# An encoder trunk on one core: the SSD mixer on a normalised residual, a scan in eight lagging steps, and aligned pools

## The chip, the cores and the metric

The kernel runs on one core of a Trainium2 chip. The metric is the device time of one execution in microseconds (us). Five engines work side by side, each through its own instructions in order: PE (TensorE, matmuls; its weight loads are listed as PEld), DVE (VectorE), ACT (ScalarE), POOL (GpSimd) and SP, which issues the transfers. An instruction waits by semaphores for what other engines make.

## The reference

Two layers on a residual `h` of 512 tokens by 1024 numbers, all in float32:

```
for i in range(2):
    h = h + 0.5 * swiglu(rmsnorm(h, g1), w_gu1, w_down1)          # FFN1, inner width 2816
    hn = rmsnorm(h, g_mix)
    h = h + (ssd_mixer(hn) if i == 0 else neighbourhood_attention(hn))
    h = h + 0.5 * swiglu(rmsnorm(h, g2), w_gu2, w_down2)          # FFN2
    h = h + sigmoid(rmsnorm(h, gp) @ w_gate) * rmsnorm(p[i] @ w_proj, gq)   # gated embedding

ssd_mixer(hn):
    z, xbc, dt = split(hn @ w_in)                  # 8256 columns
    xbc = silu(conv5(xbc) + conv_b)                # a centred convolution of 5 taps, each channel by itself
    xs, b_f, c_f, b_b, c_b = split(xbc)            # 32 heads of 64, 8 groups of 128 for B and C
    y = scan(xs, dt_f, b_f, c_f) + scan backwards(xs, dt_b, b_b, c_b) + d * xs
    return rmsnorm(y * silu(z), g) @ w_out

scan, in chunks of 128 tokens:
    y = (C B^T * exp(cum_q - cum_k), masked) @ (x dt)             # within a chunk
    states of a chunk = B^T @ (x dt * exp(cum_end - cum))
    carried = carried * exp(cum_end) + states                     # from chunk to chunk
    y += (C @ carried) * exp(cum)                                 # across chunks
```

## The kernel before

The residual lies as eight tiles `hs` of 128 channels by 512 tokens. Each product with a weight is cut into units: a unit is a piece of 128 by up to 1024 of the weight that makes 128 outputs for all tokens. `load_unit` fetches it (tile `wr`), `split_unit` splits it into a high part (`wh`, a cast on ACT, L157) and a low part (`wl`, DVE, L159), three units ahead. The operand is split in the same way by `split`: a high part on ACT (L181, L178) and a low part on DVE (L182, L179), side by side in one tile of two rows of 2048 bytes, `xa` or `md`. `gemm` adds three matmuls of 512 columns for each 128 inputs: L172 high by high, L173 high by low, L174 low by high. A unit with 8 inputs has 24 matmuls.

`Norm` feeds `h * gain` to the products, and the row factor R = 1/sqrt(mean of squares) multiplies what comes out. Squares are made on ACT (L201) and added up on POOL (L205). `SumSq.rsqrt` sums over the partitions with one matmul of ones (L209, 512 columns in plain float32), and three Newton steps on DVE work on 128 by 512 numbers (L187 to L193, L211).

In the SSD, `conv` takes the bank that a unit left in PSUM times R into SBUF (L413), multiplies the middle tap on ACT (L416), adds the four others on DVE (L420), then tanh on ACT (L423) and a product on DVE (L424). Units 6 and 7 of a group make the gate z in the same manner (L437 to L440). There are eight groups of heads, eight units to each. `scan(gi)` works on one group, and yields between its steps; the loop at the end of `ssd` runs the units of the next group (`project(gi + 1)`, with the last group the first half of the output product, `out_half`) and takes one step after each unit. Its products on PE are: C B^T (L459), transposes of xs and B (L470), the chunks' states (L518), the products within chunks (L539) and those with the carried states (L556). POOL makes x dt (L478), that with its decay (`xds`, L486), the masked products (L501) and sums (L560); DVE carries the states on (L525, L526). The Tile framework orders every engine's instructions at build time, by priority and by what it takes to be ready.

The SSD's exit adds the second half of the output product (L608 DVE, L609 POOL, L613 DVE into a new `hs` tile), and each tile goes at once into the next norm (L181, L182, L201, L205). The gated embedding is `ple` (L326 to L330). The output leaves by L835.

The tiles come from pools that lie one behind the other in each partition of SBUF: 16384 bytes for transfers' descriptors, the constants `cp` (8608 bytes), the weights `wp`, the data `bp`. All weight and data tiles of a row or more are multiples of 2048 bytes, apart from `sm` at 32 bytes.

## Time and profile before

| | |
|---|---|
| Three executions | 2464.87, 2467.52, 2467.38 us; median 2467.38 |
| Span of the profiled execution | 2462.0 us from its first to its last instruction |
| Around the span | the profiled execution has no time of its own beside its span; the median of the three lies 5.4 us above it |
| Granted TensorE clock | 0.992 on the mean |

How to read it: times in the profile are microseconds from the start of the span unless marked ns. In the list of groups, a row names line, engine, operation, the tiles written and read, the shape, the count, then busy time in us, the mean in ns, and the idle time of the engine just before with what ended it. The list of waits names who waited for whom: us in total, times, the longest. A window's row has its length, then busy time with the number of instructions (x) for PE, PEld, DVE, ACT and POOL, then the granted clock of PE, the share of the transfers' engines and GB/s. A row of the timeline has the start, the length, engine and line, and in brackets the idle time before and what ended it.

The stages by time: FFN1 to 375 us, the SSD to 987, FFN2 and the gated embedding to 1415, FFN1 of the second layer to 1785, attention to 2049, then FFN2 and the embedding.

### The profile page before, as it was taken

The numbers are of one execution on the slowest core, as the hardware profiler recorded it, in microseconds if no ns is written. First come the engines' busy times: TensorE is split into PE (matmuls) and PEld (weight loads), VectorE is DVE, ScalarE is ACT, GpSimd is POOL, SyncE is SP. The second block draws the span as 40 slices with busy tenths as digits, with TensorE's granted clock in tenths as the row PEclk, the third lists the DMA queues.
The fourth block names the chain that finished last, engine by engine and source line by source line (L and its number), as shares of the span: only waits on it lengthen the run. The fifth ranks groups of instructions, "written<-read, shape, count | busy, mean of one in ns | idle before, by whom it ended". The sixth has DMA issues, their size and how long they took to land. (4 is left out here: it accounts for less than half of the span.)

```text
span 2462.0 us, 29096 instructions
## 1 busy us (share of the span) xinstructions
PE 2395.0 (97%) x11278; PEld 1953.4 (79%) x11278; DVE 1548.6 (63%) x1983; ACT 964.0 (39%) x1545; POOL 489.4 (20%) x387
## 2 busy tenths in 40 slices
PE   8999999999999999899999999999999999999998
PEld 6888888777777778788888778888877878888887
DVE  6553448888888866645344964444478965553457
ACT  4322234555555563332234432222336753322242
POOL 2110110545555543211012111101100011110120
PEclk9999999999999999999999999999999999999999
DMA  4333342533443354233333333333434323333332
GB/s 165 96 96 100 90 126 89 167 119 122 125 123 120 122 174 129 87 101 94 96 102 95 95 93 99 99 94 92 139 120 125 112 67 99 96 94 99 99 94 77
DMA packets 89562, 266.60 MB, mean 108 GB/s; under 512 B 10944, under 2 KB 11584, under 8 KB 89424
## 3 DMA queue, kind: packets, MB, share of 16 engines
q1 hardware_dynamic: 89424, 264.75, 35.5%
q8 instruction: 88, 1.44, 0.2%
q14 instruction: 50, 0.41, 0.1%
HBM read 253.93 MB, written 10.78 MB: 108 GB/s over the span
## 5 line engine op out<-in xcount | busy, mean ns | idle before, releaser
L172 PE MATMUL ps<-xa,wh 128*128 128x512 f32 x2216 | 877.9, 396 | 17.9 <-ACT xa L181 9.2
L173 PE MATMUL ps<-xa,wh 128*128 128x512 f32 x2216 | 870.7, 393 | 3.3 <-DVE xa L182 3.3
L174 PE MATMUL ps<-xa,wl 128*128 128x512 f32 x2216 | 869.1, 392 | 0.0
L157 ACT CAST wh<-wr 128x1024 fp32r<-128x1024 f32 (+1 forms) x405 | 418.4, 1033 | 1027.2 <-PE ps L173 638.8
L159 DVE TENSOR_TENSOR wl<-wr,wh 128x1024 fp32r<-128x1024 f32 (+1 forms) x405 | 588.8, 1454 | 126.4 <-ACT wh L157 121.0
L172 PEld LDWEIGHTS ps<-xa,wh 128*128 128x128 f32 x2216 | 419.7, 189 | 108.0 <-ACT xa L181 10.6
L173 PEld LDWEIGHTS ps<-xa,wh 128*128 128x128 f32 x2216 | 419.7, 189 | 97.2 <-issue 7.1
L174 PEld LDWEIGHTS ps<-xa,wl 128*128 128x128 f32 x2216 | 418.9, 189 | 88.5 <-DVE wl L159 1.2
L172 PE MATMUL ps<-md,wh 128*128 128x512 f32 x960 | 376.6, 392 | 1.2 <-ACT md L181 1.2
L173 PE MATMUL ps<-md,wh 128*128 128x512 f32 x960 | 374.0, 390 | 1.1 <-DVE md L182 1.1
L174 PE MATMUL ps<-md,wl 128*128 128x512 f32 x960 | 373.5, 389 | 0.0
L257 POOL TENSOR_TENSOR t<-t,sc 128x512 f32<-128x512 f32 x88 | 121.2, 1379 | 1025.4 <-ACT wh L157 735.0
L205 POOL TENSOR_TENSOR sq<-sq,sq 128x512 f32<-128x512 f32 x77 | 112.0, 1454 | 595.8 <-ACT sq L201 594.6
L256 DVE TENSOR_TENSOR t<-ps,rt 128x512 f32<-128x512 f32 x88 | 60.8, 690 | 255.5 <-PE ps L174 255.5
L172 PEld LDWEIGHTS ps<-md,wh 128*128 128x128 f32 x960 | 180.2, 188 | 41.2 <-ACT md L181 2.4
L173 PEld LDWEIGHTS ps<-md,wh 128*128 128x128 f32 x960 | 180.2, 188 | 40.4 <-DVE md L182 2.3
L267 DVE SCALAR_TENSOR_TENSOR hs<-ps,hs 128x512 f32<-128x512 f32 x96 | 66.2, 690 | 229.7 <-PE ps L174 229.7
L174 PEld LDWEIGHTS ps<-md,wl 128*128 128x128 f32 x960 | 180.2, 188 | 37.6
L420 DVE SCALAR_TENSOR_TENSOR t<-t,ccw,t 128x510 f32<-128x510 f32 (+1 forms) x192 | 178.8, 934 | 5.3 <-ACT t L416 2.8
L252 DVE TENSOR_TENSOR t<-ps,rt 128x512 f32<-128x512 f32 x88 | 60.8, 691 | 127.4 <-PE ps L174 127.2
L501 POOL TENSOR_TENSOR sc<-sc,sc 128x512 f32<-128x512 f32 x64 | 106.7, 1688 | 29.8 <-ACT sc L500 29.8
L178 ACT CAST md<-t 128x512 fp32r<-128x512 f32 x88 | 54.9, 624 | 120.5 <-POOL t L257 120.5
(154 smaller groups left out, 1771.3 us busy)
## 6 DMA issues: line engine op xcount, KB each, us to landing
wr<-in_w_gu_dram SPq DMA_DIRECT2D x176, 512.0 KB, 3.6
wr<-in_w_in_dram SPq DMA_DIRECT2D x65, 512.0 KB, 3.6
wr<-in_w_dn_dram SPq DMA_DIRECT2D x64, 448.0 KB, 3.3
wr<-in_w_dn_dram SPq DMA_DIRECT2D x32, 512.0 KB, 3.5
hs<-crow SPq DMA_DIRECT2D x64, 256.0 KB, 3.6
wr<-in_w_qkv_dram SPq DMA_DIRECT2D x24, 512.0 KB, 3.6
hs<-vrow SPq DMA_DIRECT2D x64, 128.0 KB, 3.0
wr<-in_w_out_dram SPq DMA_DIRECT2D x16, 512.0 KB, 4.0
```

What stands on the lines that cost most here:

```text
L157: s.copy(out=hi[:, :n], in_=raw[:, :n])
L159: v.tensor_sub(out=lo[:, :n], in0=raw[:, :n], in1=hi[:, :n])
L172: te.matmul(out=pt, lhsT=hi[:, sl], rhs=xp[:, 0, :], start=first and k == 0, stop=False)
L173: te.matmul(out=pt, lhsT=hi[:, sl], rhs=xp[:, 1, :], start=False, stop=False)
L174: te.matmul(out=pt, lhsT=lo[:, sl], rhs=xp[:, 0, :], start=False, stop=last and k == n - 1)
L205: (v if fast else g).tensor_add(out=self.acc, in0=self.acc, in1=q)
L252: v.tensor_mul(out=gm, in0=pg, in1=R[0])
L256: v.tensor_mul(out=um, in0=pu, in1=R[0])
L257: g.tensor_mul(out=um, in0=um, in1=sg)
L267: v.scalar_tensor_tensor(out=h[d], in0=pt, scalar=0.5, in1=h[d], op0=ALU.mult, op1=ALU.add)
L420: v.scalar_tensor_tensor(out=a[:, lo:hi], in0=xb[:, lo + o:hi + o], scalar=w(j), in1=a[:, lo:hi], op0=ALU.mult, op1=ALU.add)
L501: g.tensor_mul(out=e, in0=e, in1=cbm[dr])
```

## The change

- **Pools.** The descriptors get 1024 bytes. `sm` has a pool of its own ahead of the weights (12 tiles of 32 bytes), and 2272 bytes are filled in, so that `wp` begins at byte 12288 = 6 × 2048. In before it begins at 16384 + 8608 = 24992, which is 416 beyond 12 × 2048, and every tile of weights and operands lies 416 beyond a multiple of 2048. `xa` takes its tiles from `md` (24 together, as many as before), and `sc` has 15 tiles instead of 9.
- **Row factor.** `begin` and `end` make R with the tokens on the partitions: four matmuls of one column, Newton steps on 128 by 4 numbers, and four matmuls of 128 columns that spread it out again, copied by ACT. The SSD's entry and exit and both gated embeddings use it.
- **SSD on the normalised residual.** Eight new pairs `xn` hold h · gain · R. The step-size unit and the first three units of group 0 still use the old pairs; all others use `xn`, and their `conv` and gate read the PSUM bank itself.
- **Scan.** The steps stand in a new order, one after each unit: transposes and C B^T; xds; nothing on PE; states; within chunks for heads 0 and 1; across for these; across for heads 2 and 3; within for these. The exponentials (`expo`, ACT) and masks (`masked`, POOL) are spread over the steps. The last group's y stays on the chip (`late`).
- **Exit** with three gemms ahead of the first output; **gated embedding** with its first gate after the second unit, the very last unit in two halves of the columns; **start** with half weight tiles of two units and their gemms taken in turns, the squares queued behind the last cast.

```diff
+SCRATCH = 1024
+FILL = 12288 - 10016
...
+    sp = ctx.enter_context(tc.tile_pool(name="sp", bufs=12))
+    fp = ctx.enter_context(tc.tile_pool(name="fp", bufs=1))
+    v.memset(fp.tile([P, FILL // 4], F32, name="fill")[:, :1], 0.0)
...
-    hs, t2, sc, sq = slot("hs", 8), slot("t2", 7), slot("sc", 9), slot("sq", 4)
+    hs, t2, sc, sq = slot("hs", 8), slot("t2", 7), slot("sc", 15), slot("sq", 4)
     def md(dt=F32):
-        return bp.tile([P, 2, T], dt, name=nm("md"), tag="md", bufs=16)
+        return bp.tile([P, 2, T], dt, name=nm("md"), tag="md", bufs=24)
     def xa(dt=F32R):
-        return bp.tile([P, 2, T], dt, name=nm("xa"), tag="xa", bufs=8)
+        return md(dt)
...
+        def begin(self, scale=1.0, eps=EPS):
+            pt = px_bank()
+            for c in range(NC):
+                te.matmul(out=pt[:, c:c + 1], lhsT=self.acc[:, c * P:(c + 1) * P], rhs=ones_d[:, :1],
+                          start=True, stop=True)
+            m, a, self.y = sm([NC]), sm([NC]), sm([NC])
+            v.tensor_scalar(out=m, in0=pt[:, :NC], scalar1=scale, scalar2=eps, op0=ALU.mult, op1=ALU.add)
+            newton_rsqrt(m, self.y, a)
+        def end(self):
+            pt = px_bank()
+            for c in range(NC):
+                te.matmul(out=pt[:, c * P:(c + 1) * P], lhsT=self.y[:, c:c + 1].to_broadcast([P, P]), rhs=ident,
+                          start=True, stop=True)
+            r = rt()
+            s.copy(out=r, in_=pt)
+            return r
...
     def ple(l, norm, pp, nxt):
+        halves = (slice(0, T // 2), slice(T // 2, T))
+        def gate(n, pt, R, cs):
+            u = t2()[:, cs]
+            v.tensor_mul(out=u, in0=pt, in1=R[:, cs])
+            s.activation(out=u, in_=u, func=AF.Tanh)
+            v.scalar_tensor_tensor(out=u, in0=u, scalar=1.0, in1=pp[n][:, cs], op0=ALU.add, op1=ALU.mult)
+            v.tensor_add(out=h[n][:, cs], in0=h[n][:, cs], in1=u)
         R = None
         for n in range(KD):
+            if n == KD - 1 and nxt is done:
+                w = unit()
+                for x, cs in enumerate(halves):
+                    pt = mm_bank()
+                    gemm(pt[:, cs], w, norm.pairs, cols=cs)
+                    gate(n, pt[:, cs], R, cs)
+                    (sy, s)[x].dma_start(out=out[:, n, cs], in_=h[n][:, cs])
...
-                R = norm.factor(half=True)
...
+            if n == 0:
+                norm.begin(half=True)
+                held = pt
+                continue
+            if n == 1:
+                R = norm.end()
+                gate(0, held, R, slice(0, T))
+                nxt(0)
...
-        R = norm.factor()
-        Rh = rt()
-        v.tensor_scalar(out=Rh, in0=R, scalar1=0.5, scalar2=None, op0=ALU.mult)
+        norm.begin()
+        pt0, w0 = mm_bank(), unit()
+        gemm(pt0, w0, norm.pairs[:5], last=False)
+        R = norm.end()
+        gemm(pt0, w0, norm.pairs[5:], first=False, off=5)
...
+        xn = []
+        for k in range(KD):
+            t = t2()
+            v.scalar_tensor_tensor(out=t, in0=hk[k], scalar=col(norm.gain + k), in1=R, op0=ALU.mult, op1=ALU.mult)
+            xn.append(md(F32R))
+            split(xn[k], t, None)
...
-        def conv(pt, ct, dst):
-            xb = t2()
-            v.tensor_mul(out=xb, in0=pt, in1=R)
+        def conv(src, ct, dst, raw):
+            if raw:
+                xb = t2()
+                v.tensor_mul(out=xb, in0=src, in1=R)
+                src = xb
...
-                v.scalar_tensor_tensor(out=a[:, lo:hi], in0=xb[:, lo + o:hi + o], scalar=w(j), in1=a[:, lo:hi],
+                v.scalar_tensor_tensor(out=a[:, lo:hi], in0=src[:, lo + o:hi + o], scalar=w(j), in1=a[:, lo:hi],
                                        op0=ALU.mult, op1=ALU.add)
-            th = xb
+            th = t2()
...
+                raw = gi == 0 and i < 3
+                if gi == 0 and i == 0:
+                    pt = pt0
+                else:
+                    pt = mm_bank()
+                    gemm(pt, unit(), norm.pairs if raw else xn)
                 if i < 6:
-                    conv(pt, cts[i], dsts[i])
+                    conv(pt, cts[i], dsts[i], raw)
...
+                    s.activation(out=th, in_=pt, func=AF.Tanh, scale=0.5)
+                    v.scalar_tensor_tensor(out=zt[:, i - 6, :], in0=th, scalar=1.0, in1=pt, op0=ALU.add, op1=ALU.mult)
...
+        def expo(gi, j):
+            hd, dr = 4 * gi + j // 2, j % 2
+            cb = hs()
+            sy.dma_start(out=cb, in_=crow[dr, hd:hd + 1, :].to_broadcast([P, T]))
+            e = sc()
+            for c in range(NC):
+                s.activation(out=e[:, cs(c)], in_=cb[:, cs(c)], func=AF.Relu, scale=-1.0,
+                             bias=cum[:, dr, c, hd:hd + 1])
+            s.activation(out=e, in_=e, func=AF.Exp, scale=-1.0)
+            return e
+        def scan(gi, bt, ct_, xt, zt, e0):
             h0 = 4 * gi
...
+            es = [e0]
+            def masked(j):
+                g.tensor_mul(out=es[j], in0=es[j], in1=cbm[j % 2])
...
+            es.append(expo(gi, 1))
+            yield
             xds = []
...
+            masked(0)
+            masked(1)
+            es.append(expo(gi, 2))
+            masked(2)
             yield
-            es = decay(h0)
+            es.append(expo(gi, 3))
+            masked(3)
...
+            es.append(expo(gi, 4))
+            masked(4)
+            yield
+            def within(j):
...
+            def across(j):
...
+            def gated(j, y, parts):
+                for rg, vb in parts:
                     g.tensor_add(out=y[:, rg], in0=y[:, rg], in1=vb[:, rg])
                 v.tensor_mul(out=y, in0=y, in1=zt[:, j, :])
-                sy.dma_start(out=ydram[2 * gi + j], in_=y)
                 ss.add(y)
-                yield
+                if gi == NG - 1:
+                    late.append(y)
+                else:
+                    sy.dma_start(out=ydram[2 * gi + j], in_=y)
+            y = within(0)
+            es.append(expo(gi, 5))
+            masked(5)
+            yield
+            gated(0, y, across(0))
+            es.append(expo(gi, 6))
+            masked(6)
+            yield
+            es.append(expo(gi, 7))
+            masked(7)
+            parts = across(1)
+            yield
+            gated(1, within(1), parts)
+            yield
+        late = []
...
+        e0 = expo(0, 0)
         for gi in range(NG):
             beside = project(gi + 1) if gi + 1 < NG else out_half()
-            sn = scan(gi, *cur)
-            for r in beside:
+            sn = scan(gi, *cur, e0)
+            for i, r in enumerate(beside):
                 cur = r
-                next(sn, None)
-            list(sn)
         prs = pairs_of(range(8, 16), lambda: md(F32R))
+        pts = []
+        r2 = None
         for d in range(KD):
-            pt = mm_bank()
-            gemm(pt, unit(), prs)
+            while len(pts) < 3 and d + len(pts) < KD:
+                pts.append(mm_bank())
+                gemm(pts[-1], unit(), prs)
+                if r2 is None and len(pts) == 2:
+                    ss.begin(0.5, 4.0 * EPS)
+            if r2 is None:
+                r2 = ss.end()
+            pt = pts.pop(0)
...
+    begun = [(next(todo),) + tuple(wp.tile([P, 1024], dt, name=nm(t), tag=t, bufs=b)
+                                   for t, dt, b in (("wr", F32, 4), ("wh", F32R, 3), ("wl", F32R, 3)))
+             for _ in range(2)]
...
-        if k in (1, 3):
-            load_unit()
+        if k in (0, 3):
+            for src, raw, hi, lo in begun:
+                sy.dma_start(out=raw[:, wcols[k // 3]], in_=src[:, wcols[k // 3]])
...
+    def first(pg, pu, pairs):
+        for k in range(KD):
+            for pt, (src, raw, hi, lo) in zip((pg, pu), begun):
+                gemm(pt, (hi, lo), pairs[k:k + 1], first=k == 0, last=k == KD - 1, off=k)
+        with tc.issue_after(n.last_cast.ins):
+            for k in range(KD):
+                n.count(k)
```

Three places show the order. PE in group 0 of the scan, where the products with the carried states stand (md_2609 is C, md_3198 and md_3209 the carried states, L539 the products within chunks, L172 to L174 the next unit's gemm). Before:

```order
L539 MATMUL ps_3293<-sc_3150,md_3077 64x128
L539 MATMUL ps_3293<-sc_3227,md_3077 64x128
L556 MATMUL ps_3312<-md_2609,md_3198 128x128 x2
L556 MATMUL ps_3312<-md_2609,md_3209 128x128
L556 MATMUL ps_3321<-md_2609,md_3209 128x128
L556 MATMUL ps_3321<-md_2609,md_3198 128x128 x2
L172 MATMUL ps_3334<-xa_2277,wh_3160 128x512
L173 MATMUL ps_3334<-xa_2277,wh_3160 128x512
```

After, where L650 is the product with the carried states, L629 (not in these rows) that within chunks, and L177 to L179 are the gemm:

```order
L178 MATMUL ps_3404<-md_2695,wh_3272 128x512
L179 MATMUL ps_3404<-md_2695,wl_3274 128x512
L650 MATMUL ps_3444<-md_2700,md_3309 128x128 x2
L650 MATMUL ps_3444<-md_2700,md_3320 128x128
L650 MATMUL ps_3452<-md_2700,md_3320 128x128
L650 MATMUL ps_3452<-md_2700,md_3309 128x128 x2
L177 MATMUL ps_3475<-md_2660,wh_3339 128x512
L178 MATMUL ps_3475<-md_2660,wh_3339 128x512
```

L650 no longer stands directly behind the products within chunks but behind a whole unit. In the same listing the first product of the states (L608, before L518) of groups 1 to 7 stands 49 gemm matmuls behind the last transposes, in group 0 it stands 24 behind them; before it stood 29 behind them in every group.

POOL in group 1. Before, L478 makes x dt, L486 the xds, L501 the masked products:

```order
L478 TENSOR_TENSOR md_3613<-md_3612,md_2600 128x256 x2
L486 TENSOR_TENSOR sc_3643<-md_3613,md_2600 128x256
L478 TENSOR_TENSOR md_3613<-md_3612,md_2600 128x256 x2
L478 TENSOR_TENSOR md_3631<-md_3630,md_2600 128x256 x4
L486 TENSOR_TENSOR sc_3646<-md_3613,md_2600 128x256
L486 TENSOR_TENSOR sc_3643<-md_3631,md_2600 128x256
L486 TENSOR_TENSOR sc_3646<-md_3631,md_2600 128x256
L486 TENSOR_TENSOR sc_3649<-md_3631,md_2600 128x256
L486 TENSOR_TENSOR sc_3649<-md_3613,md_2600 128x256
L501 TENSOR_TENSOR sc_3695<-sc_3695,sc_3598 128x512
L501 TENSOR_TENSOR sc_3704<-sc_3704,sc_3605 128x512
```

After, L562, L584 and L547 are the same in this order; L659 and L211 are sums of the group before:

```order
L659 TENSOR_TENSOR sc_3593<-sc_3593,hs_3527 128x384
L211 TENSOR_TENSOR sq_3463<-sq_3463,sq_3598 128x512
L562 TENSOR_TENSOR md_3652<-md_3651,md_2651 128x256 x4
L562 TENSOR_TENSOR md_3670<-md_3669,md_2651 128x256 x4
L547 TENSOR_TENSOR sc_3536<-sc_3536,sc_3687 128x512
L584 TENSOR_TENSOR sc_3744<-md_3652,md_2651 128x256
L584 TENSOR_TENSOR sc_3744<-md_3670,md_2651 128x256
L584 TENSOR_TENSOR sc_3747<-md_3652,md_2651 128x256
L584 TENSOR_TENSOR sc_3747<-md_3670,md_2651 128x256
L584 TENSOR_TENSOR sc_3750<-md_3670,md_2651 128x256
L584 TENSOR_TENSOR sc_3750<-md_3652,md_2651 128x256
L547 TENSOR_TENSOR sc_3698<-sc_3698,sc_3694 128x512
```

One masked product, which needs C B^T from DVE, now stands ahead of the xds, and all of x dt ahead of both.

DVE at the SSD's entry. Before, the Newton steps of R and then the first convolution:

```order
L159 TENSOR_TENSOR wl_2658<-wr_2493,wh_2656 128x1024
L191 TENSOR_TENSOR sc_2584<-rt_2585 128x512
L192 SCALAR_TENSOR_TENSOR sc_2584<-sc_2584,sc_2583 128x512
L193 SCALAR_TENSOR_TENSOR rt_2585<-sc_2584,rt_2585 128x512
L348 TENSOR_SCALAR rt_2598<-rt_2585 128x512
L358 TENSOR_TENSOR t_2604<-ps_2550,rt_2585 64x512
L413 TENSOR_TENSOR t_2643<-ps_2612,rt_2585 128x512
L159 TENSOR_TENSOR wl_2699<-wr_2551,wh_2697 128x1024
L413 TENSOR_TENSOR t_2684<-ps_2653,rt_2585 128x512
L420 SCALAR_TENSOR_TENSOR t_2645<-t_2643,ccw,t_2645 128x510
```

After, the end of the small Newton steps, then the new pairs (L429 the product, L184 the low part), then the first product with R of a raw unit (L486):

```order
L199 SCALAR_TENSOR_TENSOR sm_2600<-sm_2599,sm_2600 128x4
L423 TENSOR_TENSOR t_2655<-ps_2562,rt_2640 64x512
L429 SCALAR_TENSOR_TENSOR t_2658<-hs_78,cst,rt_2640 128x512
L429 SCALAR_TENSOR_TENSOR t_2663<-hs_79,cst,rt_2640 128x512
L184 TENSOR_TENSOR md_2660<-t_2658,md_2660 128x512
L184 TENSOR_TENSOR md_2665<-t_2663,md_2665 128x512
L184 TENSOR_TENSOR md_2695<-t_2693,md_2695 128x512
L486 TENSOR_TENSOR t_2703<-ps_2613,rt_2640 128x512
L164 TENSOR_TENSOR wl_2719<-wr_2563,wh_2717 128x1024
L494 SCALAR_TENSOR_TENSOR t_2705<-t_2703,ccw,t_2705 128x510
```

Sixteen instructions stand between R and the first convolution where none stood; eleven of them are not shown here.

More of the change, by code (lines that the diff above doesn't have):

```diff
@@ L91, in trunk @@
     warm = cp.tile([P, 1], F32, name="warm")
-    s.activation(out=warm, in_=ones_d[:, 0:1], func=AF.Silu)
     ident = msk[:, M_ID:M_ID + P]
@@ L165, in unit, with gemm @@
         return ready.pop(0)
-    def gemm(pt, w, pairs, first=True, last=True, off=0):
+    def gemm(pt, w, pairs, first=True, last=True, off=0, cols=slice(0, T)):
         hi, lo = w
@@ L171, in gemm @@
             sl = slice((off + k) * P, (off + k + 1) * P)
[L172 to L174 removed]
+            te.matmul(out=pt, lhsT=hi[:, sl], rhs=xp[:, 0, cols], start=first and k == 0, stop=False)
+            te.matmul(out=pt, lhsT=hi[:, sl], rhs=xp[:, 1, cols], start=False, stop=False)
+            te.matmul(out=pt, lhsT=lo[:, sl], rhs=xp[:, 0, cols], start=False, stop=last and k == n - 1)
     def split(dst, src, gain):
         if gain is None:
[L178 removed]
+            cast = s.copy(out=dst[:, 0, :], in_=src)
             v.tensor_sub(out=dst[:, 1, :], in0=src, in1=dst[:, 0, :])
         else:
[L181 removed]
+            cast = s.activation(out=dst[:, 0, :], in_=src, func=AF.Copy, scale=gain)
             v.scalar_tensor_tensor(out=dst[:, 1, :], in0=src, scalar=gain, in1=dst[:, 0, :],
                                    op0=ALU.mult, op1=ALU.subtract)
+        return cast
     def newton_rsqrt(m, y, a):
@@ L225, in prep @@
             pr = self.alloc()
-            split(pr, h[k], col(self.gain + k))
+            self.last_cast = split(pr, h[k], col(self.gain + k))
             self.pairs.append(pr)
@@ L232, in count, with factor, begin, end @@
             self.ss.add(h[k], fast=k == KD - 1)
-        def factor(self, half=False):
+        def factor(self):
+            return self.ss.rsqrt()
+        def begin(self, half=False):
             if half:
-                return self.ss.rsqrt(4.0, 4.0 * EPS)
-            return self.ss.rsqrt()
-    def ffn(norm, nxt, between=lambda: None):
+                self.ss.begin(4.0, 4.0 * EPS)
+            else:
+                self.ss.begin()
+        def end(self):
+            return self.ss.end()
+    def ffn(norm, nxt, between=lambda: None, first=None):
         R = [None]
         mids = {}
+        held = []
         def gate_up(f):
-            pg = mm_bank()
+            pg, pu = mm_bank(), mm_bank()
+            if first and f == 0:
+                first(pg, pu, norm.pairs)
+                held.append((f, pg, pu))
+                return
             gemm(pg, unit(), norm.pairs)
-            pu = mm_bank()
             gemm(pu, unit(), norm.pairs)
@@ L479, in scan @@
                                  in1=bc4(dtk[:, c, dr * 32 + h0:dr * 32 + h0 + 4]))
+            cbm = []
+            for dr in range(2):
+                pt = px_bank()
+                for c in range(NC):
+                    te.matmul(out=pt[:, cs(c)], lhsT=bt[:, dr, cs(c)], rhs=ct_[:, dr, cs(c)], start=True, stop=True)
+                m = sc()
+                mk = (M_LE, M_GE)[dr]
+                v.tensor_mul(out=m.rearrange("p (c q) -> p c q", c=NC), in0=pt.rearrange("p (c q) -> p c q", c=NC),
+                             in1=msk[:, mk:mk + P].unsqueeze(1).to_broadcast([P, NC, P]))
+                cbm.append(m)
+            es.append(expo(gi, 1))
+            yield
             xds = []
@@ L539, in scan @@
                             te.matmul(out=pd[hh * 64:(hh + 1) * 64, cs(c)], lhsT=xdt[c][:, o:o + 64],
-                                      rhs=both[hh][dr][:, cs(c)], start=dr == 0 and c == 0,
+                                      rhs=es[4 * j + 2 * hh + dr][:, cs(c)], start=dr == 0 and c == 0,
                                       stop=dr == 1 and c == NC - 1)
@@ L568, in pairs_of @@
             for k in ks:
-                yt = t2()
-                sy.dma_start(out=yt, in_=ydram[k])
+                if k < 14:
+                    yt = t2()
+                    sy.dma_start(out=yt, in_=ydram[k])
+                else:
+                    yt = late[k - 14]
                 pr = alloc()
@@ L847, in trunk @@
         n.prep(k, False)
-        if k in (1, 3):
-            split_unit()
-    for k in range(KD):
-        n.count(k)
+        if k in (0, 3):
+            for src, raw, hi, lo in begun:
+                sl = wcols[k // 3]
+                s.copy(out=hi[:, sl], in_=raw[:, sl])
+                last_lo = v.tensor_sub(out=lo[:, sl], in0=raw[:, sl], in1=hi[:, sl])
+    def first(pg, pu, pairs):
[5 more added lines that the diff above has]
+                n.count(k)
     for i in range(stop):
@@ L857, in trunk @@
         if w == 0:
-            ffn(n, nxt)
+            ffn(n, nxt, first=first if i == 0 else None)
         elif w == 1:
```

78 lines of the change are left out of this document (24 added, 54 removed).

## The prediction

> **What bounds the kernel now.** I read the head of the page first, then the waits of PE, then windows and the timeline at the places they name.
>
> ```profile
> span 2462.0 us, 29096 instructions
> PE 2395.0 (97%) x11278; PEld 1953.4 (79%) x11278; DVE 1548.6 (63%) x1983; ACT 964.0 (39%) x1545; POOL 489.4 (20%) x387
> ...
> L172 PE MATMUL ps<-xa,wh 128*128 128x512 f32 x2216 | 877.9, 396 | 17.9 <-ACT xa L181 9.2
> L172 PE MATMUL ps<-md,wh 128*128 128x512 f32 x960 | 376.6, 392 | 1.2 <-ACT md L181 1.2
> ...
> PE ps L556 <- DVE md L526: 23.0, 14, 2.0
> PE ps L518 <- POOL sc L486: 12.2, 14, 1.4
> PE ps L172 <- ACT xa L181: 9.2, 4, 4.5
> ```
>
> PE is the bound. L172 runs 2216 + 960 = 3176 times, L173 and L174 as often: 9528 matmuls of 512 columns. The rest can only come from three places: how long one matmul takes, the waits, and the clock. Windows (PE first, then PEld, DVE, ACT, POOL, the clock) price one matmul and one group of the SSD scan:
>
> ```profile
> 2060.00:2400.00 340.00, 340.00 (x1500) 281.17 (x1499) 167.74 (x170) 108.76 (x137) 44.62 (x33) 1.00 0.33 97
> 448.23:514.39 66.16, 61.14 (x325) 49.68 (x324) 55.08 (x65) 34.48 (x69) 31.62 (x28) 0.95 0.40 122
> 514.39:577.80 63.41, 58.39 (x325) 47.46 (x324) 55.14 (x65) 34.48 (x69) 32.91 (x29) 1.00 0.41 125
> 464.27:471.10 6.83, 5.84 (x18) 4.97 (x19) 6.83 (x10) 4.83 (x12) 2.63 (x2) 0.50 0.40 118
> ```
>
> In a stretch of gemms alone PE takes 340/1500 = 226.67 ns each, so 9528 × 0.22667 = 2160 us of the span. A group of the scan takes 63.4 us, or 66.2 where 6.83 us of it run at clock 0.50.
>
> **The waits in the scan.** One group:
>
> ```profile
> 450.25 2.29 PE L518 MATMUL ps<-sc,md 128*128 128x256 f32 x8 [1.42 <-POOL sc L486]
> 452.85 0.70 PE L518 MATMUL ps<-sc,md 128*128 128x256 f32 x2 [0.32 <-POOL sc L486]
> 463.27 0.71 PE L556 MATMUL ps<-md,md 128*128 128x128 f32 x4 [2.00 <-DVE md L526]
> ```
>
> L518 and L556 wait 23.0 + 12.2 = 35.2 us, 5.03 in each of seven groups. After the change the states' products stand two units behind their transposes from the second group on. POOL's work in between:
>
> ```profile
> L501 POOL TENSOR_TENSOR sc<-sc,sc 128x512 f32<-128x512 f32 x56 | 94.4, 1706 | 29.8 <-ACT sc L500 29.8
> L478 POOL TENSOR_TENSOR md<-md,md 128x256 f32<-128x256 f32 x55 | 48.5, 908 | 77.2 <-ACT md L474 77.2
> L486 POOL TENSOR_TENSOR sc<-md,md 128x256 f32<-128x256 f32 x42 | 33.9, 831 | 0.0
> L474 ACT COPY md<-ps 128x512 f32<-128x512 f32 x25 | 12.8, 592 | 0.0
> ```
>
> The last transposes are followed by a copy (0.6), two xdt products (1.8), one mask (1.7, itself waiting for DVE's masked product) and six xds (5.0): 9.1 us, against 48 gemm matmuls, 10.9 us: no wait, with 1.8 us to spare. In the first group only one unit (5.4 us) lies between; the first pair of xds is ready by then, the next two come 1.7 us apart for products of 0.4, so 2.5 us stay. The carried-state products (L556, L650 after) now stand a whole unit behind the within-chunk products and wait for nothing. Waits: −35.2 + 2.5 = −32.7; between −35.2 and, if POOL's lag stays everywhere, −23.0. PE's number of changes between scan products and gemm stays (about seven a group), +0.5.
>
> **The clock.** The stretch at 0.50 follows the group's 2.00 + 1.28 us of waiting and costs 66.16 − 63.41 = 2.75 us; it comes in every second group, four times. Without the waits three go and the first group's may stay: −8.2, between −11 and 0. The Trainium skill ("TensorE: Matmul & The Clock Gate", Part 1) gives a free-running window of 3413 ns, after an idle one of which the clock halves; the 6.83 us seen is two of these, and the trace agrees.
>
> **Alignment.** All tiles of the weight and data pools start, in before, 416 bytes beyond a multiple of 2048, that is 32 beyond one of 128; after it, on a multiple of 2048 (the sizes ahead of them, from the code). No row shows an aligned moving operand. What rows show is when a matmul costs more than its columns:
>
> ```profile
> 467.56 0.63 PE L173 MATMUL ps<-xa,wh 128*128 128x512 f32 x1
> 469.27 0.63 PE L174 MATMUL ps<-xa,wl 128*128 128x512 f32 x1
> ...
> 380.44 1.02 PE L209 MATMUL ps<-sq,ones_d 128*128 128x512 f32 x2
> ...
> L209 PE MATMUL ps<-sq,ones_d x2: 591/592/592, 380.4 to 380.9; 128*128 128x512 f32 x2
> ```
>
> The first two rows are the first and the last of five matmuls in a row in the stretch at clock 0.50: 1.71/4 = 0.427 us from one to the next, so 213.5 ns at full clock if columns were all. The fast matmul has 13 ns on top of that, and 226.67 is 17/16 of 213.33 (the 512 columns at 2.4 a ns that 0.427 us at half clock come to) to the hundredth. The plain float32 L209 pair, 1.02 − 0.59 = 0.43 us from one to the next, twice 213.5 and no more, also has nothing on top. Both take in 512 columns at half the pace. So the extra sixteenth appears only where the operand is read at the full pace: a limit of its supply, not of the array. A row of 2048 bytes that starts 32 beyond a multiple of 128 touches 17 pieces of 128 bytes, an aligned one 16. That fits without a free number; a fixed start-up of the read of just a sixteenth fits too, and would stay. Bounds: 0 and −13.3 ns for each of 9528, 0 to −127 us. I take the near end of the half-pace rows, with their 1.7 to 2 ns on top of 2 × 213.3 for an instruction: 215.3, so −11.3 × 9528 = −108. About 3.5 us of that are lost where PE waits for others (the SSD's exit, the cold start): −104. The Trainium skill ("TensorE: Matmul & The Clock Gate", Back-to-back issue gap) gives N/2.4 + 2.5 ns, an estimate of 215.8 for 512 columns; the trace's 226.67 is not that, and by it the term would be −104 before the loss.
>
> **Convolution from PSUM.** It drops the product with R: 41 × 684 ns and 14 × 682 in seven groups, 5.4 us of DVE in each, and reads the bank four times on DVE, once on ACT.
>
> ```profile
> L420 DVE SCALAR_TENSOR_TENSOR t<-t,ccw,t 128x510 f32<-128x510 f32 x82 | 86.0, 1049 | 3.8 <-ACT t L416 2.8
> L420 DVE SCALAR_TENSOR_TENSOR t<-t,ccw,t 128x511 f32<-128x511 f32 x82 | 72.5, 884 | 1.5
> L413 DVE TENSOR_TENSOR t<-ps,rt 128x512 f32<-128x512 f32 x41 | 28.0, 684 | 20.7 <-PE ps L174 20.5
> L543 DVE SCALAR_TENSOR_TENSOR sc<-md,cst,ps 128x512 f32<-128x512 f32 x14 | 10.3, 738 | 0.0
> L437 DVE TENSOR_TENSOR t<-ps,rt 128x512 f32<-128x512 f32 x14 | 9.5, 682 | 0.0
> ```
>
> The same kind of instruction with a PSUM operand takes 738 (L543) beside 884 and 1049 for taps with both operands in SBUF. DVE, 55 of a group's 63.4 us now, falls to 49.7, or to 44 if the 24 taps take L543's time. PE hides it: worth 0 by itself, and a cover for the scan's steps. The bank is held 4 to 5 us longer, of five that are filled 5.4 us apart. The Trainium skill ("VectorE: DVE Perf Modes", Rules for kernel authors) lets an operation read the bank at plain speed or advises a copy to SBUF first where many follow, which speaks against this change; by it DVE would stay near 55 us a group, still under PE's 58.4, and the sum would be the same. L543's row speaks against it.
>
> **Entry of the SSD.**
>
> ```profile
> 377.25 0.75 DVE L182 SCALAR_TENSOR_TENSOR xa<-hs,cst,xa 128x512 fp32r<-128x512 f32 x1
> 382.68 0.68 DVE L211 TENSOR_SCALAR sc<-ps 128x512 f32<-128x512 f32 x1
> 391.14 0.69 DVE L193 SCALAR_TENSOR_TENSOR rt<-sc,rt 128x512 f32<-128x512 f32 x1
> ...
> L191 DVE TENSOR_TENSOR sm<-sm 128x8 f32<-128x8 f32 x24 | 3.8, 159 | 0.1
> ```
>
> The Newton steps shrink from 382.7–391.8 to 12 × 0.16, six us sooner; then 8 × 0.75 + 8 × 0.69 = 11.5 us for the normalised pairs stand on DVE ahead of the convolution, needed by the fourth unit of the group and ready about when it starts; the weights' low part for that unit is queued behind them. The broadcast in small matmuls costs PE 1 us more than the L209 pair. +2, between 0 and +6.
>
> **Other places.**
>
> ```profile
> 993.54 0.50 PE L172 MATMUL ps<-xa,wh 128*128 128x512 f32 x1 [1.67 <-ACT xa L181]
> 999.55 0.80 PE L172 MATMUL ps<-xa,wh 128*128 128x512 f32 x1 [4.49 <-ACT xa L181]
> 991.65 1.08 DVE L613 TENSOR_TENSOR hs<-sc,t 128x512 f32<-128x512 f32 x1 [1.17 <-POOL t L609]
> 997.66 1.08 DVE L613 TENSOR_TENSOR hs<-sc,t 128x512 f32<-128x512 f32 x1 [1.15 <-POOL t L609]
> 1421.55 0.50 PE L172 MATMUL ps<-xa,wh 128*128 128x512 f32 x1 [1.60 <-ACT xa L181]
> ```
>
> The SSD's exit is a chain DVE L613, ACT, POOL L205, POOL L609 of 6.01 us a tile against a gemm of 5.44; its order on POOL and DVE is the same after, and R comes no sooner: +1 (0 to +3). The gated embedding gets R sooner, so the 1.6 us and the 3.4 us at half clock behind it (1.7) go: −2.6 with the extra broadcast; the second one pays the broadcast alone, +1. The last scan group loses one stall, −1; the split last gemm −0.3; the rewritten start 0 (−2 to +3), since sums of squares queue ahead of the third gemm.
>
> **Sum** on the profiled span: −32.7 + 0.5 − 8.2 + 2 + 1 − 2.6 + 1 − 1 − 0.3 = −40; with alignment −144, so 2318. The runs' median, 2467.38, lies 5.4 above the span, which I add again: **2323 us**.
>
> **Rivals.**
> - No gain from alignment (the sixteenth is a start-up): 2467.4 − 40 = 2427, range 2405 to 2450. For it: not one aligned row. Against it: nothing on top at half pace, and exactly 17/16.
> - The waits move rather than go (POOL late by its L501 ahead of the xds, DVE late at the entry), and alignment gives nothing: −40 shrinks to −10 or nothing, 2455 to 2468.
> - Slower: DVE becomes the bound of the groups because PSUM taps are dear. It decides, with nothing from alignment, where DVE's 49.7 us a group pass the present mean period, 64.8: 26 PSUM-reading operations each 0.58 us dearer than today's mean tap of 0.97, so 1.55. L543's 738 ns and L437's 682 speak against it. At 1.7 us a tap it gives (49.7 + 26 × 0.73 − 64.8) × 7 = +27: 2495.
>
> **Chances.** Alignment with the scan's gain 0.53 (own range 2297 to 2345), no alignment 0.35, waits moved 0.08, DVE bound 0.04. The range 2297 to 2450 leaves out about 0.13 in all. A difference under 0.2% (5 us) can't be told from none: faster 0.93, same 0.03, slower 0.04.
>
> **What would show it.** A stretch of FFN gemms: 1500 matmuls in 323 us, not 340. In a scan group: no wait on the states above 0.3 us, PE at clock 1.00 throughout, the taps at 0.74 and DVE under 50 us. At the entry: fewer than 3 us of waiting before the fourth unit. The exit: still one wait of about 4.5. Wrong it would be if gemms kept 226.7 ns, or if PE waited for POOL's xds in every group.

## The result and the profile after

The changed kernel takes 2410.45 us in the median (2409.42 to 2412.87) beside 2467.45 for the kernel before in the same comparison: a ratio of 0.9771, 95% interval 0.9757 to 0.9785, so 57 us saved. The forecast was 2323 us. The direction is right, the size is not: the term for alignment, −104 us, did not come at all, and the scan gave more than its terms say.

The head of the page, PE's longest waits, and two kinds of windows (a stretch of gemms alone, then three groups of the scan from one first states' product to the next), all of the kernel after:

```profile
span 2408.5 us, 29115 instructions
PE 2379.1 (99%) x11358; PEld 1953.1 (81%) x11358; DVE 1441.3 (60%) x1940; ACT 965.9 (40%) x1557; POOL 461.7 (19%) x387
...
PE ps L177 <- ACT md L186: 9.2, 5, 4.0
PE ps L177 <- ACT wh L990: 5.8, 1, 5.8
PE ps L215 <- DVE sq L211: 4.0, 1, 4.0
PE ps L178 <- DVE md L187: 3.2, 6, 0.8
...
2010.00:2350.00 340.00, 340.00 (x1500) 281.25 (x1499) 166.95 (x169) 106.79 (x135) 46.63 (x33) 1.00 0.33 98
...
512.09:568.96 56.87, 56.87 (x326) 47.69 (x324) 42.40 (x56) 34.10 (x70) 29.30 (x29) 1.00 0.43 140
568.96:625.80 56.84, 56.84 (x326) 47.69 (x324) 42.39 (x56) 34.07 (x70) 29.28 (x29) 1.00 0.45 140
625.80:682.66 56.86, 56.86 (x326) 47.69 (x324) 42.42 (x56) 34.09 (x70) 29.31 (x29) 1.00 0.45 139
```

The stretch of gemms has the same 1500 matmuls in 340 us as before: 226.67 ns each, to the hundredth. The waits for POOL's xds and DVE's states are gone from the list. A group takes 56.9 us, PE is busy in all of it and the clock is at 1.00 throughout; before, groups took 63.4 and 66.2 in turn. DVE is down from 55 to 42.4 us a group.

Where the 53.5 us between the spans (2462.0 to 2408.5) come from is read by counting gemm matmuls in the two traces and comparing the times at which the same number has started: at the 1536th, in the first FFN, the kernel after leads by 0.3 us; at the 1848th, as the first scan group begins, by 1.5; at the 3096th, at the end of the seventh group, by 56.9; at the 3552nd, at the SSD's exit, by 51.3; and at the last one by 52.4. So the seven groups gave 55.3 us, the SSD's last group and exit took 5.5 back, and all else together gave 3.7.

### The profile page after: what moved, and what is told of

Same layout as the page of the kernel before. It is cut to its first block, busy times and chain, and to the rows that moved or that the text cites. A ratio compares the mean times of both kernels' runs of the same rounds, so it can differ in the third digit from the quotient of the medians.

```text
span 2408.5 us, 29115 instructions
## 1 busy us (share of the span) xinstructions
PE 2379.1 (99%) x11358; PEld 1953.1 (81%) x11358; DVE 1441.3 (60%) x1940; ACT 965.9 (40%) x1557; POOL 461.7 (19%) x387
## 4 chain that ended last, share of the span: by engine, by line
PE 57%; DVE 4%; ACT 1%; POOL 1%; issue 0%; DMA 0%; SPq 0%; POOLq 0%; DVEq 0%
PE ps L178 18%; PE ps L177 18%; PE ps L179 18%; PE ps L910 1%; DVE wl L164 1%; PE ps L867 1%; PE ps L901 1%; DVE md L187 0%; DVE md L355 0%; POOL t L740 0%; DVE sc L198 0%; PE ps L773 0%; PE ps L893 0%; DVE sc L197 0%; DVE rt L199 0%
## 5 line engine op out<-in xcount | busy, mean ns | idle before, releaser
L177 PE MATMUL ps<-md,wh 128*128 128x512 f32 x3184 | 1252.2, 393 | 15.2 <-ACT md L186 9.2
L178 PE MATMUL ps<-md,wh 128*128 128x512 f32 x3184 | 1243.0, 390 | 3.3 <-DVE md L187 3.2
L179 PE MATMUL ps<-md,wl 128*128 128x512 f32 x3184 | 1241.8, 390 | 0.6 <-DVE wl L164 0.6
L162 ACT CAST wh<-wr 128x1024 fp32r<-128x1024 f32 (+1 forms) x403 | 416.5, 1034 | 1036.2 <-PE ps L178 655.5
L177 PEld LDWEIGHTS ps<-md,wh 128*128 128x128 f32 x3184 | 599.4, 188 | 147.2 <-ACT md L186 12.8
L178 PEld LDWEIGHTS ps<-md,wh 128*128 128x128 f32 x3184 | 599.5, 188 | 133.8 <-DVE md L187 7.1
L179 PEld LDWEIGHTS ps<-md,wl 128*128 128x128 f32 x3184 | 599.3, 188 | 125.2 <-DVE wl L164 1.1
L211 POOL TENSOR_TENSOR sq<-sq,sq 128x512 f32<-128x512 f32 x77 | 110.0, 1428 | 599.8 <-ACT sq L207 598.3
L494 DVE SCALAR_TENSOR_TENSOR t<-ps,ccw,t 128x510 f32<-128x510 f32 (+1 forms) x180 | 134.0, 744 | 3.2 <-ACT t L490 0.3
L547 POOL TENSOR_TENSOR sc<-sc,sc 128x512 f32<-128x512 f32 x64 | 96.2, 1518 | 71.4 <-ACT sc L537 71.3
L535 ACT ACTIVATE sc<-hs,md 128x128 f32<-128x128 f32 x256 | 82.4, 397 | 1.7 <-DMA hs<-crow 1.7
L184 DVE TENSOR_TENSOR md<-t,md 128x512 fp32r<-128x512 f32 x96 | 66.8, 700 | 21.5 <-ACT md L183 21.1
L186 ACT ACTIVATE md<-hs,cst 128x512 fp32r<-128x512 f32 x64 | 45.9, 722 | 61.8 <-DVE hs L744 26.1
L187 DVE SCALAR_TENSOR_TENSOR md<-hs,cst,md 128x512 fp32r<-128x512 f32 x64 | 53.3, 843 | 14.6 <-ACT md L186 14.6
L562 POOL TENSOR_TENSOR md<-md,md 128x256 f32<-128x256 f32 x64 | 44.1, 723 | 80.6 <-ACT md L558 80.6
```

The lines of the kernel that those rows point to most:

```text
L162: s.copy(out=hi[:, :n], in_=raw[:, :n])
L177: te.matmul(out=pt, lhsT=hi[:, sl], rhs=xp[:, 0, cols], start=first and k == 0, stop=False)
L178: te.matmul(out=pt, lhsT=hi[:, sl], rhs=xp[:, 1, cols], start=False, stop=False)
L179: te.matmul(out=pt, lhsT=lo[:, sl], rhs=xp[:, 0, cols], start=False, stop=last and k == n - 1)
L184: v.tensor_sub(out=dst[:, 1, :], in0=src, in1=dst[:, 0, :])
L211: (v if fast else g).tensor_add(out=self.acc, in0=self.acc, in1=q)
```

## The experiments

**The rate of the matmul.** This kernel has only rows of 64 matmuls, each row of one kind: W holds eight pieces of weights, xr an operand on a multiple of 2048 bytes. A last row, L91, has plain float32 operands of 512 columns.

```diff
+    te.matmul(out=p0, lhsT=W[i % 8], rhs=xr[:, 0:512], ...)          # L73
+    te.matmul(out=p1, lhsT=W[i % 8], rhs=xr[:, 8:520], ...)          # L76, 32 bytes on
+    te.matmul(out=p2[:, :384], lhsT=W[i % 8], rhs=xr[:, 0:384], ...) # L79
+    te.matmul(out=p3, lhsT=W[0], rhs=xr[:, 0:512], ...)              # L82
+    te.matmul(out=p4[:, :256], lhsT=W[i % 8], rhs=xr[:, 0:256], ...) # L85
+    te.matmul(out=p5[:64], lhsT=W[i % 8][:, :64], rhs=xr[:, 0:512], ...) # L88
```

> Leaves out the whole computation: seven rows of 64 matmuls, each row of one kind, on one operand. Theory 1 (a fixed cost per float32r matmul of 32 columns' time, 13.3 ns): 226.7 ns at 512 columns whether the operand starts on a multiple of 2048 or 32 bytes beyond one, 173.3 ns at 384 columns. Theory 2 (a share of the columns, 17 for 16, whatever the address): 226.7 and 226.7, but 170.0 at 384. Theory 3 (alignment after all, with something else in the kernel in its way): 213 to 216 on the multiple, 226.7 beside it. Theory 4 (the change of weights): 213 to 216 where the weights have 64 columns instead of 128, or where they are the same piece each time.

The timeline (start, length of the whole row) and the length of one matmul:

```profile
28.02 14.67 PE L73 MATMUL p<-xr,wr 128*128 128x512 f32 x64
42.52 15.10 PE L76 MATMUL p<-xr,wr 128*128 128x512 f32 x64
57.46 11.28 PE L79 MATMUL p<-xr,wr 128*128 128x384 f32 x64
68.58 14.71 PE L82 MATMUL p<-xr,wr 128*128 128x512 f32 x64
83.12 7.83 PE L85 MATMUL p<-xr,wr 128*128 128x256 f32 x64
90.79 14.87 PE L88 MATMUL p<-xr,wr 128*64 128x512 f32 x64
105.50 54.24 PE L91 MATMUL p<-x,w 128*128 128x512 f32 x126
...
L73 PE MATMUL p<-xr,wr x64: 389/389/389, 28.0 to 42.3; 128*128 128x512 f32 x64
L79 PE MATMUL p<-xr,wr x64: 334/334/346, 57.5 to 68.4; 128*128 128x384 f32 x64
L85 PE MATMUL p<-xr,wr x64: 277/283/283, 83.1 to 90.7; 128*128 128x256 f32 x64
```

From one to the next, (row − one) / 63: 226.7 ns at 512 columns on the multiple of 2048, 173.7 at 384 (most single steps are 173), 119.8 at 256. Against the columns' time at 2.4 a ns (213.3, 160.0, 106.7) each has 13.1 to 13.7 ns on top: a fixed cost, as theory 1 has it. The share of theory 2 would be 170.0 at 384. Theory 3 is out too, since the row on the multiple of 2048 takes 226.7. The same weights each time (L82, 227 ns) and weights of half the width (L88, 230 ns) do not help, against theory 4. The plain float32 row takes 429 ns a matmul, twice 213.3 and 2.4. The row that starts 32 bytes on took 233 ns, 7 more, which theory 1 does not have; the kernel before, whose operands all lie like that, ran at 226.67 and so does the next one, so I can't say what that row shows.

**Alignment alone.**

```diff
-    fp = ctx.enter_context(tc.tile_pool(name="fp", bufs=1))
-    v.memset(fp.tile([P, FILL // 4], F32, name="fill")[:, :1], 0.0)
```

> The changed kernel without the filling of 2272 bytes, so that weights and operands lie at 10016, 32 beyond a multiple of 128, as before. If alignment is worth nothing: 2410 us, within 3. If it helps somewhere else than in PE's rate (DVE, ACT, transfers): over 2416.

2412.63 us (2410.67 to 2413.52), 0.9781 of before (0.9765 to 0.9797), beside 0.9771 with the filling: the intervals lie on each other. The stretch of gemms:

```profile
2010.00:2350.00 340.00, 340.00 (x1499) 281.25 (x1498) 166.98 (x168) 107.15 (x136) 46.71 (x33) 1.00 0.33 98
```

1499 in place of 1500 in the same window, and the time is within the 3 us that were expected. Where the tiles start is worth nothing here.

**Scan and convolution apart.** The scan's old steps in the changed kernel:

```diff
-        def scan(gi, bt, ct_, xt, zt, e0):   # eight steps
+        def scan(gi, bt, ct_, xt, zt):       # the kernel before's, with late[] for the last group
```

> The changed kernel with the scan in its old steps (states one unit after the transposes, carried products directly behind the products within chunks); convolution from PSUM, pairs, pools as changed. Theory A (the lag removes the waits): the waits on POOL's xds and DVE's states come back, 25 to 35 us of idle time, with what they cost beside it and the half clock 40 to 55 us: 2450 to 2465. Theory B (the shorter DVE queue removes them, the steps' order nothing): 2410 to 2420.

And the old pairs with the convolution from a copy in SBUF:

```diff
-                raw = gi == 0 and i < 3
+                raw = True
-                    gemm(pt, unit(), norm.pairs if raw else xn)
+                    gemm(pt, unit(), norm.pairs)
+                    v.tensor_mul(out=zz, in0=pt, in1=R)   # the gate z reads zz
```

> The changed kernel with the old pairs throughout and the convolution and gate reading a copy in SBUF that was multiplied by R; scan in its new steps. Theory A: DVE goes back to some 55 us a group under PE's 57, no wait of more than 0.5 us comes back in the scan, and the entry is rid of the new pairs: 2406 to 2416. Theory B: the waits come back for want of DVE's time: over 2435.

And both undone:

> The changed kernel with both the old scan steps and the old convolution and pairs: what stays is the pools, the row factor in two halves, the exit, the gated embedding, the start. If the scan's and the convolution's parts add up (34.8 and 46.3 us lost when one is undone), 2410 + 81 = 2492. If each alone lifts the same waits only in part and the two are needed together: near the kernel before, 2460 to 2472.

| | convolution old | convolution from PSUM |
|---|---|---|
| scan old | 2470.47 (ratio 1.0011, 1.0002 to 1.0021) | 2445.22 (0.9911, 0.9896 to 0.9926) |
| scan in eight steps | 2456.70 (0.9957, 0.9942 to 0.9972) | 2410.45 (0.9771, 0.9757 to 0.9785) |

With the scan old the time lies between what the two theories gave. With the convolution old it is theory B's, but with other waits than those of the kernel before. With both old the parts do not add up to 2492: the time is near the kernel before, and the rest of the change (factor, exit, embedding, start) gives nothing there. From that corner the convolution alone gives 25 us, the scan alone 14, and the two together 60: 21 more than the sum. PE's waits with the scan old, then with the convolution old:

```profile
PE ps L633 <- DVE md L603: 16.9, 12, 2.0
...
PE ps L595 <- POOL sc L563: 3.1, 1, 3.1
...
PE ps L550 <- ACT md L554: 27.2, 7, 4.6
...
PE ps L550 <- DVE sc L629: 3.8, 4, 2.3
```

With the old scan, POOL's xds are late only once (12.2 us in 14 waits before, and 12.1 in 14 with both old), while the states' wait is still there: 16.9 of 23.0. So the convolution alone removes POOL's wait, and the lag is needed for DVE's. With the old convolution a wait that the kernel before did not have takes their place: the transposes (L550) wait 4.3 to 4.6 us in six groups for ACT's copy of the bank that they need. The mean granted clock is 0.990 in both, beside 0.997 in the kernel after, so half clock behind the waits has a part in both losses. ACT and DVE there, around 556 us:

```profile
561.13 0.81 ACT L484 ACTIVATE t<-t,ccw 128x512 f32<-128x512 f32 x1
565.85 0.63 ACT L491 ACTIVATE t<-t 128x512 f32<-128x512 f32 x1 [3.91 <-DVE t L488]
566.39 1.54 ACT L554 COPY md<-ps 128x512 f32<-128x512 f32 x3
...
556.00 1.47 PE L550 MATMUL ps<-msk,md 128*128 128x128 f32 x12
567.01 1.12 PE L550 MATMUL ps<-msk,md 128*128 128x128 f32 x4 [4.52 <-ACT md L554]
```

ACT's copies (L554) stand behind a convolution's tanh (L491), and that waits 3.91 us for the taps (L488) on DVE: the copies come 10.4 us after the transposes. In the kernel after the same copies come 5.9 us after them, and the gemm between covers that:

```profile
554.27 0.63 ACT L497 ACTIVATE t<-t 128x512 f32<-128x512 f32 x1 [3.69 <-DVE t L494]
554.81 2.03 ACT L558 COPY md<-ps 128x512 f32<-128x512 f32 x4
...
548.88 1.47 PE L554 MATMUL ps<-msk,md 128*128 128x128 f32 x12
555.44 0.65 PE L554 MATMUL ps<-msk,md 128*128 128x128 f32 x4
```

The four taps just ahead of that tanh are no slower than in the kernel after: 3.10 us in both. What is late is DVE's queue. The sum that makes y (L629, and L633 after) stands in it ahead of these taps, and needs PE's products within chunks (L625, and L629 after). The last of these products, the sum and the taps, then a window from the first states' product to about where the sum starts; first with the old convolution, then in the kernel after:

```profile
548.52 1.97 PE L625 MATMUL ps<-sc,md 128*64 128x128 f32 x32
555.96 0.74 DVE L629 SCALAR_TENSOR_TENSOR sc<-md,cst,ps 128x512 f32<-128x512 f32 x1
562.66 3.10 DVE L488 SCALAR_TENSOR_TENSOR t<-t,ccw,t 128x510 f32<-128x510 f32 x4
519.21:556.00 36.79, 36.79 (x221) 30.73 (x220) 34.92 (x46) 19.61 (x38) 10.24 (x8) 1.00 0.43 129
...
541.41 1.97 PE L629 MATMUL ps<-sc,md 128*64 128x128 f32 x32
544.11 0.74 DVE L633 SCALAR_TENSOR_TENSOR sc<-md,cst,ps 128x512 f32<-128x512 f32 x1
551.08 3.10 DVE L494 SCALAR_TENSOR_TENSOR t<-ps,ccw,t 128x510 f32<-128x510 f32 x4
512.09:544.00 31.91, 31.91 (x200) 26.77 (x199) 25.45 (x35) 18.30 (x36) 12.47 (x9) 1.00 0.44 146
```

With the old convolution DVE takes the sum up 5.5 us behind the end of the products, in the kernel after 0.7 us. It was busy for 34.9 of the 36.8 us ahead of the sum, beside 25.5 of 31.9. Over the whole group (519.21 to 582.07) it is busy for only 52.9 of 62.9 us: the average hides the stretch in which DVE is full.

**Which part of the convolution it is.** First, one more operation on DVE that nobody waits for:

```diff
+            if not raw:
+                v.tensor_mul(out=spare[:, :T], in0=src, in1=R)
```

> The changed kernel with one more DVE operation a convolution, off its chain: a product of the PSUM bank with R into a spare tile that nobody reads, after the taps (six a group, 4.1 us). If the waits that the old convolution brings back come from DVE's load: waits of PE in the scan, 2420 or more. If they come from its place on the chain, or from taps with two SBUF operands: 2409 to 2414.

2411.71 us (0.9782, 0.9768 to 0.9795): nothing. Some 4 us more of DVE's time a group find room, and the sum still starts 0.7 us behind the products. The old convolution adds more, 10.5 us a group (42.4 to 52.9), so this run does not rule out a larger load. Second, a copy ahead of ACT's middle tap, with the taps still on PSUM:

```diff
+                mid = a
+                v.tensor_scalar(out=a, in0=src, scalar1=1.0, scalar2=None, op0=ALU.mult)
-            s.activation(out=a, in_=src, func=AF.Identity, scale=w(2), ...)
+            s.activation(out=a, in_=mid, func=AF.Identity, scale=w(2), ...)
```

> The changed kernel with a DVE copy of the bank ahead of ACT's middle tap; the four taps still read PSUM, so POOL is not disturbed. If the old convolution's loss comes from ACT having to wait for DVE at the head of each convolution, with the scan's copies queued behind it on ACT: the wait of the transposes for ACT's copy comes back, 2435 or more. If it comes from the taps' slower operands or the load alone: 2409 to 2416.

2419.92 us (0.9810, 0.9797 to 0.9824): between the two expectations, 9 us of the 46 (7 beside the changed kernel's 2412.45 further on), from single waits rather than one in every group. Third, a copy that the four taps read, while ACT reads the bank; and fourth, with ACT on the copy as well:

```diff
+                tap = t2()
+                v.tensor_scalar(out=tap, in0=src, scalar1=1.0, scalar2=None, op0=ALU.mult)
-                v.scalar_tensor_tensor(out=a[:, lo:hi], in0=src[:, lo + o:hi + o], ...)
+                v.scalar_tensor_tensor(out=a[:, lo:hi], in0=tap[:, lo + o:hi + o], ...)
```

> The changed kernel with a DVE copy of the bank to SBUF that the four taps read, so that they have two SBUF operands again; ACT's middle tap still reads the bank. If the taps' slowing beside POOL is what brings the waits back: 2435 or more. If it takes that together with ACT waiting for the copy: 2410 to 2420.

> The same with ACT's middle tap reading the copy too: the old convolution but for its factor R, with the new pairs and the gate from PSUM. If copy at the head and slow taps together make the loss: 2440 to 2457, and PE waits for ACT's copies of the transposes in every group. If it is the pairs or the gate: under 2425.

2457.91 us (0.9966, 0.9956 to 0.9977) and 2453.69 (0.9948, 0.9931 to 0.9964): the whole loss, as expected of slow taps, and the same wait of the transposes for ACT in six groups. Taps and xds: first the third kernel's taps from 380 to 442 us, where POOL is busy for 1.6 us in all; then from 442 to 800 us the third kernel, and the kernel after (its taps are L494, its xds L584):

```profile
L498 DVE SCALAR_TENSOR_TENSOR t<-t,ccw,t 128x510 f32<-128x510 f32 x12 | 8.9, 745 | 0.1
...
L498 DVE SCALAR_TENSOR_TENSOR t<-t,ccw,t 128x510 f32<-128x510 f32 x71 | 71.5, 1007 | 6.2 <-ACT t L494 5.4
L588 POOL TENSOR_TENSOR sc<-md,md 128x256 f32<-128x256 f32 x36 | 34.1, 977 | 0.0
...
L494 DVE SCALAR_TENSOR_TENSOR t<-ps,ccw,t 128x510 f32<-128x510 f32 x77 | 57.2, 743 | 1.4 <-ACT t L490 0.3
L584 POOL TENSOR_TENSOR sc<-md,md 128x256 f32<-128x256 f32 x42 | 27.1, 680 | 0.0
```

Beside POOL's work a tap takes 1007 ns on the mean with two operands in SBUF and 743 with one in PSUM (over 511 columns 939 and 745). With POOL nearly idle the same tap with two operands in SBUF takes 745: the operand in SBUF is not slow by itself, it is slow beside POOL. POOL's xds take 977 and 680 beside them, but its x dt go the other way, 652 and 738, so the rows show the gain for DVE more plainly than for POOL. The Trainium skill ("SBUF — State Buffer", SBUF: two separate sides) has DVE operations with two SBUF inputs and GpSimd's reads exclude each other; the taps' rows and the xds agree.

So the slow taps fill DVE's queue in the stretch where POOL works. In the third kernel too the sum of y starts about 5 us behind the products (0.7 in the second), and the lateness reaches PE through the tanh and the copies. The second and the fourth kernel differ in what the four taps read, the bank or the copy, and in one tile more for the copy: 34 us. No run has slow taps without a copy, so what they would cost by themselves is not shown.

**Exit and start.** The SSD's exit as before:

```diff
+        r2 = ss.rsqrt(0.5, 4.0 * EPS)
-            while len(pts) < 3 and d + len(pts) < KD: ...
+            pt = mm_bank()
+            gemm(pt, unit(), prs)
```

> The changed kernel with the old exit of the SSD: the factor in one matmul and eight Newton steps of full width, one gemm ahead. If the new exit gives its factor some 6 us sooner and only the later last product of the scan eats that: 2414 to 2419. If the new exit itself is what costs the 6 us that the stage lost: 2404 to 2407.

2412.80 us (2407.30 to 2414.96; 0.9778, 0.9759 to 0.9796): on neither expectation, and not to be told from the changed kernel. The new exit is not what costs the 5.5 us; that the last product of the scan now stands later among the gemms, with fewer of them behind it, is what remains; that is argued and not shown. The exit's product with the factor on DVE:

```diff
-            g.tensor_mul(out=u, in0=u, in1=r2)
+            v.tensor_mul(out=u, in0=u, in1=r2)
```

> The changed kernel with the exit's product with the factor (L740) on DVE instead of POOL. If the exit's 6 us a tile are the loop over POOL's two operations: the loop falls below the gemm's 5.44, the waits of 3.5 and 4.0 us shrink to one of about 3, and the stretch at half clock goes: 2400 to 2404. If DVE's own queue is the limit: 2408 to 2413.

> The kernel of e7 again, in more rounds and beside the changed kernel: if the exit's loop over POOL costs what its first runs showed, 3 to 6 us under the changed kernel, in every pair; if that was the clock's chance, within 2 us of it.

> The changed kernel itself, to stand beside e11 on the same chip: 2409 to 2413.

2406.40 us at first, then 2405.00 (0.9757, 0.9743 to 0.9770) beside the changed kernel's 2412.45 (0.9786, 0.9771 to 0.9801). The intervals of these two just miss each other, and single times overlap (2403.13 to 2410.71, and 2409.41 to 2417.47): probably a version that beats both kernels, by 0.3% at most. The 2400 to 2404 that were expected did not come. PE's waits at the end of the SSD, after and then in this version:

```profile
942.22 0.49 PE L177 MATMUL ps<-md,wh 128*128 128x512 f32 x1 [3.47 <-ACT md L186]
948.24 0.79 PE L177 MATMUL ps<-md,wh 128*128 128x512 f32 x1 [4.01 <-ACT md L186]
...
942.62 0.79 PE L177 MATMUL ps<-md,wh 128*128 128x512 f32 x1 [3.61 <-ACT md L186]
```

One of the two large waits is gone, as expected; of the 6.8 us at half clock behind them 3.4 stay. The first sum of squares one unit later on PE:

```diff
+            if R[0] is None and first:
+                with tc.issue_after(mm.ins):
+                    R[0] = norm.factor()
```

> The changed kernel with the first sum of squares (L215) standing on PE behind the third unit instead of the second. The wait of 4.05 us on POOL's sums and the half clock behind it (eight matmuls, 1.6 us) go: 2404 to 2406. Rival: the activations of the first two units then come late and the banks run out: 2410 or more.

2411.34 us (2410.91 to 2411.97): no gain, and for neither reason. The wait on POOL's sums is gone, but PE waits for the third unit's weights in the same stretch (ACT's cast L162, 2.0 us, DVE's low parts, 1.3), and the half clock follows just the same.

## Why the prediction was wrong, and where it was right

- **Alignment, −104: the step that failed.** The 13.3 ns on top of the columns were read rightly from the rows at half clock, and they are there. That they are a read of 17 pieces in place of 16, and go with the address, was chosen over the start-up that the text names beside it; the ratio 17/16 "without a free number" was what decided, and it was a coincidence of 512 columns: at 384 columns the ratio measured is near 13/12, at 256 near 9/8, on aligned operands. What showed in its place is a fixed 13.3 ns for every float32r matmul at full clock, wherever this kernel's tiles start; what makes it, and why it does not show at half clock, stays open. The row of half-length matmuls that the trace of before held, the attention's scores of 256 columns, was not used, and it could not have told a start-up from an extra piece either; only a chip run could. The rival without alignment, 2427, range 2405 to 2450, holds the result; its middle is 17 us too slow, by the waits and the clock below.
- **The waits, −32.7: the mechanism right, the price too small.** They went, the first group's too (−2.5 that I kept). But each cost more than the idle time shown: a group at full clock went from 63.41 to 56.86 us, 6.55, where 5.02 of idle time were listed. A waiting matmul's idle time is counted from the modelled end of the one before, 379 ns after its start for the states' product, while the next could have started 215 ns after it (twelve of them take 2.75 us in the kernel after). Over seven groups that is some 10.7 us that stood in no row of idle time.
- **The clock, −8.2: −10.9**, since the first group's stretch at half clock went too. The prediction has the clock halve after an idle window and finds the trace in agreement; only the length of the stretch agrees. In the 3.41 us before the clock fell at 464.27, half the length of the stretch, PE was not idle throughout: it was busy for 1.1.
- **Convolution, 0: wrong together with the scan.** It is worth 25 us with the old scan, and without it the new scan loses 46. I priced it as DVE time under PE's cover, on the average of a group. In the stretch ahead of the sum of y there is no cover: with taps at 1007 ns in place of 743 DVE takes the sum up about 5 us behind PE's products in place of 0.7, and that passes on in order: the sum, the next taps, tanh on ACT, ACT's copies of the transposes, PE. I named the row of taps and drew from it only busy time.
- **Pairs at the entry, +2: −1.2.** One wait of 0.65 us, for the low part of the weights that are queued behind the new pairs, as the step says.
- **Exit +1 and last group −1: together +5.5.** The chain's loop and the wait of about 4 were as told; that a scan which lags ends its last group later was not priced.
- **Embeddings −2.6 and +1, start 0, changes of products +0.5:** −2.7 in the first embedding, +1.3 in the second, −0.3 at the start. The start's wait is 4.0 us for POOL's sums, which a stretch at half clock follows, paid by a first matmul that starts 2.9 us sooner.
- **From span to time, +5.4:** in every execution on record the time is 1.7 to 2.0 us above the span. The rest of the 5.4, some 3.5 us, is that the profiled execution of the kernel before was faster than the median; it is no cost around the span.

Of the rivals, DVE as the bound and the waits that move did not come; with the old convolution the waits do move, to ACT's copies behind DVE's late queue, at 2457.

## What to carry to other kernels

A ratio that fits a mechanism is not yet one: where two explanations of a fixed excess give the same number at the only size in the trace, the forecast belongs to the one that changes nothing, until a size that tells them apart has been measured. An engine's busy time over a whole period says what it can carry, not when its results come, and it hides the stretch in which the engine is full: follow the in-order queues from the operation that gets slower to the one for which the bound engine waits. And idle time before a pipelined engine's instruction understates a wait by about the overlap of two instructions.

## What was not expected of the hardware

- A float32r matmul at full clock costs its columns plus some 13.3 ns, at 256, 384 and 512 columns alike, with the same weights or new ones; the plain float32 one of 512 columns (429 ns) has 2.4 ns on top of twice its columns. So the same work in fewer and longer matmuls should be cheaper, which is an estimate from these rows: 9528 of them carry 127 us here. The Trainium skill ("TensorE: Matmul & The Clock Gate", Back-to-back issue gap) has 2.5 ns on top, which no float32r row of this case shows.
- One SBUF operand less in a DVE operation made it faster by a quarter beside POOL (1007 to 743 ns; 745 with two SBUF operands where POOL is nearly idle), and a kernel that is bound by PE faster by 1.9% (2457.91 with the taps on a copy, 2410.45 on the bank; a DVE operation more in each convolution, off its chain, cost nothing).
